# Attention sweep of an encoder layer: maxima turned in another PSUM bank and later in the group, one-over-sums products moved to the last group of four, and VectorE's order written out

## The chip, the cores and the metric

The kernel runs on one core of one Trainium2 chip. The metric is the device time of one execution in microseconds, taken as the median of several runs. The profile is that of one further execution. Its engines are called PE (TensorE), DVE (VectorE), ACT (ScalarE), POOL (GpSimd) and SP (SyncE, which issues most DMAs).

## The reference, cut to what matters

The program is one layer of an encoder: grouped-query attention over 1024 tokens, and then a mixture of 32 experts. The change lies in the attention alone.

```
qkv = x @ w_qkv                       # 16 query heads, 4 key/value heads, 64 wide
q, k = rope(rms_norm(q)), rope(rms_norm(k))
def query_block(q_blk):               # 128 queries at a time
    s = einsum('bqkgd,bskd->bkgqs', q_blk, k) * scale
    p = softmax(s, axis=-1)
    return einsum('bkgqs,bskd->bqkgd', p, v)
x = layer_norm(ALPHA * x + o @ w_o)
x = layer_norm(ALPHA * x + moe_ffn(x))   # top 4 of 32 experts
```

## The kernel before

The program has four stages: the projections to q, k and v (up to about 162 us), the attention sweep (to about 519 us), the output projection with layer norm and router (to about 760 us), and the experts.

The sweep runs over 32 groups n = 4i + g: block i of 128 queries (0 to 7), key/value head g (0 to 3), four query heads each. A group goes through eight steps k = 0 to 7, one for each tile of 128 keys. In step k PE makes the scores of this tile (`st`, two matmuls, function `probs`): the first multiplies the keys with the queries, the second multiplies a tile `q2` that holds the queries and, in four more rows, the negated maxima of each query. ACT takes the exponential into `pt` (L444), and POOL adds the `pt` of a group up into `acc` (L448), all but the last, which DVE adds (`late_sum`, L452).

The maxima must be known a group ahead. So in the same step PE makes half of a tile of scores the other way round (`sc`, function `scores`) for group n + 2, and DVE reduces each whole tile to its maxima `nm` (L434), four reductions in a group. `maxima_a` (L147, L148) turns the `nm` of group n + 1 with a PE transposition into a PSUM tile `tpm`, and a DVE product writes it into the four rows of `q2`. `maxima_b` (L153) has ACT copy the queries into `q2`.

After step 3 of a group, PE multiplies the `pt` of the group before with the values (`pv`, 32 matmuls into `po`), and ACT copies `po` out to `ot` (`close_a`, L469). In groups with g = 1 and 2 PE also turns half of the next block's queries (`stack_q`, tile `tpq`, L163) ahead of `pv`; ACT and DVE write the result into `qs`. In groups with g = 0 PE adds the four `acc` of the block before over the keys (`scale_a`, tile `su`) after `pv`, and DVE makes one-over-sums from it (L479 to L484, ending in `rr`). In groups with g = 1 PE spreads `rr` over the partitions (`scale_b`, tile `rb`, after steps 5 and 7), DVE multiplies `ot` with it (L492), and SP writes `ot` to memory (`od`, L494).

PSUM is full: `st` has two banks, `sc` two tiles of two banks, and one bank each is left for the tag `tp` and the tag `po`. In the tag `tp` stand `tpm`, `tpq`, `su` and `rb`, one at a time: each waits until the last reader of the one before is done. `po` has its bank alone.

PE's order in the sweep is written out by hand (`manual_schedule`, the loop below); DVE's, ACT's, POOL's and SP's orders are set by a scheduler when the program is built. Every matmul stands at L55.

Of the kernel before, what the change touches and what calls it, by code (L numbers as in the profile page):

```python
# [9 lines left out]
F32 = mybir.dt.float32  # L10
# [10 lines left out]
P = 128  # L21
# [6 lines left out]
HD = 64  # L28
# [17 lines left out]
def trunk_kernel(ctx: ExitStack, tc: tile.TileContext, x, w_qkv, q_norm, k_norm, w_o,  # L46
                 lnm_g, lnm_b, lnf_g, lnf_b, r_w, r_b, w_gu, b_gu, w_dn, b_dn,
                 rope_c, rope_s, out):
    nc = tc.nc
# [4 lines left out]
    def mm(o, lhsT, rhs, start=True, stop=True):  # L54
        nc.tensor.matmul(o, lhsT=lhsT, rhs=rhs, start=start, stop=stop)  # L55
# [49 lines left out]
    vn = p_kv.tile([P, NT, NKV, HD], F32, name="vn")  # L105
# [35 lines left out]
        if s == 7:  # L141
            nc.vector.tensor_reduce(nms[0], nms.pop("h"), AX.X, ALU.min)

    def maxima_a(n, ps):

        tp = ps.tile([P, 4, P], F32, tag="tp", name=f"tpm{n}")
        nc.tensor.transpose(tp[0:4, 0, :], nms.pop(n).bitcast(F32), ident)  # L147
        nc.vector.tensor_tensor(q2s[n % 3][HD:HD + 4], tp[0:4, 0:1, :].to_broadcast([4, 4, P]),  # L148
                                ident[0:4, 0:4, None].to_broadcast([4, 4, P]), ALU.mult)

    def maxima_b(n):
        i, g = divmod(n, NKV)
        nc.scalar.copy(q2s[n % 3][0:HD], qs[i][0:HD, 4 * g:4 * g + 4, :].bitcast(F32))  # L153

    def stack_q(i, h, ps):

        if h == 0:
            qs[i] = p_xq.tile([P, NH, P], F32R, tag="cols", bufs=2, name=f"qs{i}")
        qv = qs[i][:, 8 * h:8 * h + 8, :].rearrange("p (j a) t -> p j a t", a=2)
        tp = ps.tile([P, 4, P], F32, tag="tp", name=f"tpq{i}_{h}")  # L160
        for c in range(4):
            j = 4 * h + c
            nc.tensor.transpose(tp[:, c, :], ql[i][:, j * P:(j + 1) * P], ident)  # L163
        odd = p_xq.tile([P, 4, P], F32R, tag="odd", name=f"odd{i}_{h}")
        nc.scalar.copy(qv[0:HD, :, 0, :], tp[0:HD])
        nc.scalar.copy(odd[HD:P], tp[HD:P])
        nc.vector.tensor_tensor(qv[HD:P, :, 0, :], tp[0:HD], qv[0:HD, :, 0, :].bitcast(F32), ALU.subtract)
        nc.vector.tensor_tensor(qv[HD:P, :, 1, :], tp[HD:P], odd[HD:P].bitcast(F32), ALU.subtract)
        nc.scalar.copy(qv[0:HD, :, 1, :], odd[HD:P].bitcast(F32))
# [4 lines left out]
    with tc.tile_pool(name="p1", bufs=1, side="right", reuse_waits="tile") as p1, \  # L174
# [34 lines left out]
        def proj(i, k, j):  # L209
            hi, lo = xTs[i]  # L210
            sl = slice(j * 512, (j + 1) * 512)
            mm3(qkvs[i][j], hi[:, k, :], lo[:, k, :], wh[k][:, sl], wl[k][:, sl], k == 0, k == KD - 1)

        def open_qkv(i):
            t = {j: ps1.tile([P, 512], F32, tag=f"qkv{j}", name=f"qkv{i}_{j}") for j in (0, 2, 1)}
            qkvs[i] = [t[j] for j in range(3)]
# [4 lines left out]
        pe_order = ExitStack()  # L221
# [76 lines left out]
        def take_q(i, j):  # L298
            if j == 0:
                qcs[i] = rot("wr", [P, QKV], 3)  # L300
            qc = qcs[i][:, j * 512:(j + 1) * 512]
            if i == NT - 1 and j == 1:
                nc.scalar.copy(qc, qkvs[i][j])
                norms(qc, sums[i][:, 8 * j:8 * j + 8])
                return
            norms(qkvs[i][j], sums[i][:, 8 * j:8 * j + 8])
            nc.scalar.copy(qc, qkvs[i][j])
# [13 lines left out]
        for i in range(NT):  # L321
            k0 = (KD, late)[i] if i < 2 else 0
            if i > 1:
                open_qkv(i)
            for k in range(k0, KD):
                proj(i, k, 2)
            if 1 < i < NT - 1:
                turn_x(i + 1)
            norm_k(i)
            if i == NT - 1:  # L330
                stack_q(0, 0, ps1)
                stack_q(0, 1, ps1)
            for k in range(k0, KD):
                proj(i, k, 0)
                if i == NT - 1 and k % 2 == 1:
                    first_scores(k // 2, ps1)
            take_q(i, 0)
            if i == 0:
                take_q(i, 1)
            turn_k(i)  # L340
            if i == 0:
                turn_x(2)
            norm_q(i, 0)
            for k in range(k0, KD):
                proj(i, k, 1)
                if i == NT - 1 and 0 < k < 5:
                    first_scores(k + 3, ps1)
                if i == NT - 1 and k == 6:
                    maxima_a(0, ps1)
                    maxima_b(0)  # L350
            if i > 0:
                take_q(i, 1)
            norm_q(i, 1)
            if i == 1:
                in_order.close()
# [61 lines left out]
    with tc.tile_pool(name="p2", bufs=1, side="right", reuse_waits="tile") as p2, \  # L417
# [4 lines left out]
        pts, po, ot, sc, accs, rrs = [{} for _ in range(6)]  # L422
        NG = NT * NKV
# [30 lines left out]
        def pv(n):  # L454

            i, g = divmod(n, NKV)
            po[n] = ps_o.tile([P, 2, P], F32, tag="po", name=f"po{n}")
            for k in range(NT):
                for a in range(2):
                    mm(po[n][a * HD:(a + 1) * HD].rearrange("p j t -> p (j t)"), vn[:, k, g, :],  # L460
                       pts[n, k][:, 2 * a * P:(2 * a + 2) * P], k == 0, k == NT - 1)
            for k in range(NT):
                del pts[n, k]

        def close_a(n):
            i, g = divmod(n, NKV)
            if g == 0:
                ot[i] = p2.tile([P, KD, P], F32, tag="ot", bufs=2, name=f"ot{i}")
            nc.scalar.copy(ot[i][:, 2 * g:2 * g + 2, :], po.pop(n))  # L469

        def scale_a(i):

            su = ps_t.tile([P, 4, P], F32, tag="tp", name=f"su{i}")
            for m in range(4):
                for g in range(NKV):
                    mm(su[g * NE:(g + 1) * NE, 0, :], which[:, m].rearrange("p r m -> p (r m)"),
                       accs[NKV * i + g][:, m * P:(m + 1) * P], m == 0, m == 3)
            rs = p2.tile([P, P], F32, tag="rs", bufs=1, name=f"rs{i}")
            nc.vector.reciprocal(rs, su[:, 0, :])  # L479
            hi = p2.tile([P, P], F32R, tag="rh", bufs=1, name=f"rh{i}")  # L480
            nc.vector.tensor_copy(hi, rs)
            nc.vector.scalar_tensor_tensor(rs, hi.bitcast(F32), low, rs, ALU.mult, ALU.subtract)
            rrs[i] = p2.tile([P, KD, P], F32R, tag="rr", bufs=1, name=f"rr{i}")
            nc.vector.tensor_tensor(rrs[i], rs[:, None, :].to_broadcast([P, KD, P]),  # L484
                                    col.rearrange("p g j -> p (g j)")[:, :, None].to_broadcast([P, KD, P]), ALU.mult)
# [39 lines left out]


        pe_order = ExitStack()
        pe_order.enter_context(tc.manual_schedule(engines={mybir.EngineType.PE}))
        for n in range(NG + 1):
            i, g = divmod(n, NKV)  # L530
            for k in range(NT):
                if k == (6 if n == 0 else 2) and n + 1 < NG:
                    maxima_a(n + 1, ps_t)
                if n < NG:
                    probs(n, k)
                if n == 0:
                    for m in range(2):
                        scores(1 + k // 4, k % 4, m)
                elif n + 2 < NG:
                    scores(n + 2, k // 2, k % 2)  # L540
                if n < NG and i + 1 < NT and g == 0 and k == 6:
                    load_q(i + 1)
                if k == (7 if n == 0 else 3) and n + 1 < NG:
                    maxima_b(n + 1)
                if k == 3 and n > 0:
                    if g in (1, 2) and i + 1 < NT:
                        stack_q(i + 1, g - 1, ps_t)
                    if n < NG - 1:
                        late_sum(n - 1)
                    pv(n - 1)  # L550
                    close_a(n - 1)
                    if g == 0:
                        scale_a(i - 1)
                if i > 0:
                    if (g, k) == (1, 5) or n == NG and k == 5:
                        scale_b(i - 1, 0)
                    if (g, k) == (1, 7) or n == NG and k == 7:
                        scale_b(i - 1, 1)
            if i in (2, 3) and g == 2:
                load_o(i - 2)  # L560
            if i == 4 and g == 2:
                load_xr(0)
# [790 lines left out]
    for i in range(NT // 2):  # L1353
        f = slot(order[(len(seq) + 1 + i) % len(order)], f"fs{i}")
# [13 lines left out]
    with tc.tile_pool(name="gen", bufs=1, side="right", reuse_waits="tile") as gp, \  # L1368
# [5 lines left out]
        with tc.For_i(0, n_blk, 1) as b:  # L1374
# [33 lines left out]
            for n in range(4):  # L1408
                w = gp.tile([P, KD, 512], F32, tag="gw", bufs=2, name=f"gwg{n}")
                nc.sync.dma_start(w, w_gu[ds(ev, 1), :, n * 512:(n + 1) * 512].rearrange("o (k p) n -> p (o k) n", p=P))  # L1410
                ps = gps.tile([P, 512], F32, tag="gu", bufs=2, name=f"ggu{n}")
# [6 lines left out]
            for n in range(2):  # L1418
                w = gp.tile([P, KD, 512], F32, tag="gw", bufs=2, name=f"gwd{n}")
                nc.sync.dma_start(w, w_dn[ds(ev, 1), :, n * 512:(n + 1) * 512].rearrange("o (k p) n -> p (o k) n", p=P))  # L1420
                ps = gps.tile([P, 512], F32, tag="gu", bufs=2, name=f"gy{n}")
# [87 lines left out]
```

## Time and profile before

| | us |
|---|---|
| median of 3 runs | 2079.25 |
| lowest and highest of them | 2078.68, 2081.83 |
| profiled execution, its own time | 2075.34 |
| its span, first to last instruction | 2073.5 |
| PE busy in the span | 2011.8 (97%) |
| DVE busy in the span | 1601.8 (77%) |

The profiled execution is a little faster than the three timed runs. Its span is what the trace covers; its time has 1.8 us more around it. Busy shares of PE hide little waits, since a matmul's end is modelled; the starts of consecutive matmuls and the idle time shown in brackets tell more.

### The profile page before, as it was taken

How to read it: one execution, taken by the hardware profiler on the slowest of the kernel's cores; microseconds unless marked ns; L12 is line 12 of the kernel's file. 1: busy time of each engine (PE TensorE's matmuls, PEld its weight loads, DVE VectorE, ACT ScalarE, POOL GpSimd, SP SyncE). 2: the span in 40 equal slices, each digit the busy share in tenths (PEclk: the TensorE clock that was granted, in tenths of full speed). 3: DMA queues.
4: the chain of work that ended last, by engine and by line, in shares of the span. 5: the costliest groups of instructions: out<-in, count | busy, mean ns of one | idle time of the engine just before them, and what ended most of it. 6: DMA issues, size and time to landing. Idle time of an engine off the chain costs nothing. (4 is left out here: it accounts for less than half of the span.)

```text
span 2073.5 us, 28716 instructions
## 1 busy us (share of the span) xinstructions
PE 2011.8 (97%) x10691; PEld 1419.5 (68%) x10691; DVE 1601.8 (77%) x1649; ACT 1282.0 (62%) x1566; POOL 538.2 (26%) x373
## 2 busy tenths in 40 slices
PE   8998999999997999999999999999999999999997
PEld 6775666665675666666666767767777677677774
DVE  6647777776887877767777878878878788887894
ACT  5655655654554656566666766667667676676774
POOL 1216777775144211111102111101021121010100
PEclk9999999999998999999999999999999999999999
DMA  5216000000645777888788898978989889789875
GB/s 174 72 62 178 31 32 21 32 21 21 228 149 211 276 287 271 298 294 291 285 315 312 347 338 304 377 289 342 338 319 354 310 315 367 284 346 337 329 314 183
DMA packets 106352, 500.44 MB, mean 241 GB/s; under 512 B 16001, under 2 KB 17026, under 8 KB 73442
## 3 DMA queue, kind: packets, MB, share of 16 engines
q1 hardware_dynamic: 87360, 447.02, 56.0%
q0 software_dynamic: 16000, 50.90, 9.0%
q8 instruction: 85, 1.39, 0.3%
q10 hardware_dynamic: 2850, 0.66, 0.2%
q14 instruction: 57, 0.47, 0.1%
HBM read 457.05 MB, written 41.49 MB: 240 GB/s over the span
## 5 line engine op out<-in xcount | busy, mean ns | idle before, releaser
L55 PE MATMUL gu<-wh,xTh 128*128 128x512 f32 x1024 | 415.3, 406 | 1.0 <-ACT xTh L63 1.0
L55 PE MATMUL gu<-wh,xTl 128*128 128x512 f32 x1024 | 410.1, 400 | 0.0
L55 PE MATMUL gu<-wl,xTh 128*128 128x512 f32 x1024 | 401.9, 393 | 0.0
L1299 POOL DMA_INDIRECT fd<-y,mi x32 | 79.1, 2472 | 655.4 <-ACT y L1298 655.4
L448 POOL TENSOR_TENSOR acc<-acc,pt 128x512 f32<-128x512 f32 x152 | 211.8, 1394 | 78.3 <-ACT pt L444 68.7
L55 PEld LDWEIGHTS gu<-wh,xTh 128*128 128x128 f32 x1024 | 193.3, 189 | 42.4 <-ACT xTh L63 1.7
L55 PEld LDWEIGHTS gu<-wl,xTh 128*128 128x128 f32 x1024 | 193.3, 189 | 39.6 <-issue 0.2
L55 PEld LDWEIGHTS gu<-wh,xTl 128*128 128x128 f32 x1024 | 193.7, 189 | 38.8 <-issue 3.6
L55 PE MATMUL yp<-wl,aTh 128*128 128x512 f32 x512 | 204.2, 399 | 0.4 <-DVE wl L612 0.4
L55 PE MATMUL yp<-wh,aTh 128*128 128x512 f32 x512 | 201.6, 394 | 0.0
L55 PE MATMUL yp<-wh,aTl 128*128 128x512 f32 x512 | 199.7, 390 | 0.0
L434 DVE TENSOR_REDUCE nm<-sc 128x1 fp32r<-128x1024 f32 x124 | 150.6, 1221 | 50.5 <-PE sc L55 49.5
L444 ACT ACTIVATE pt<-st 128x512 f32<-128x512 f32 x256 | 149.4, 596 | 55.9 <-PE st L55 46.3
L598 POOL DMA_INDIRECT xg<-xd,mi x32 | 53.4, 1670 | 298.5 <-PE tpx L1136 288.9
L55 PE MATMUL qkv<-wh,xT 128*128 128x512 f32 x384 | 123.9, 403 | 2.6 <-ACT xT L63 1.4
L55 PEld LDWEIGHTS yp<-wh,aTh 128*128 128x128 f32 x512 | 96.2, 188 | 33.6 <-ACT act L1180 14.3
L55 PE MATMUL po<-pt,vn 128*64 128x256 f32 x1024 | 117.6, 382 | 0.0
L55 PE MATMUL st<-qs,kT_hi 128*128 128x512 f32 x256 | 112.5, 440 | 2.9 <-ACT pt L444 2.2
L55 PEld LDWEIGHTS yp<-wl,aTh 128*128 128x128 f32 x512 | 96.3, 188 | 21.9 <-DVE wl L612 1.2
L55 PEld LDWEIGHTS yp<-wh,aTl 128*128 128x128 f32 x512 | 96.1, 188 | 19.5
L55 PE MATMUL st<-q,kT_lo 128*128 128x512 f32 x256 | 102.2, 399 | 1.3 <-DVE q L148 1.3
L55 PE MATMUL sc<-kT_hi,qs 128*128 128x512 f32 x256 | 101.9, 404 | 1.0 <-DVE nm L434 0.8
(520 smaller groups left out, 4159.0 us busy)
## 6 DMA issues: line engine op xcount, KB each, us to landing
w0g<-in_expert_w_gate_up SPq DMA_DIRECT2D x8, 1024.0 KB, 7.1
w1g<-in_expert_w_gate_up SPq DMA_DIRECT2D x8, 1024.0 KB, 7.6
w2g<-in_expert_w_gate_up SPq DMA_DIRECT2D x8, 1024.0 KB, 9.6
w3g<-in_expert_w_gate_up SPq DMA_DIRECT2D x8, 1024.0 KB, 8.6
w4g<-in_expert_w_gate_up SPq DMA_DIRECT2D x8, 1024.0 KB, 6.9
w5g<-in_expert_w_gate_up SPq DMA_DIRECT2D x8, 1024.0 KB, 7.4
w6g<-in_expert_w_gate_up SPq DMA_DIRECT2D x8, 1024.0 KB, 6.5
w7g<-in_expert_w_gate_up SPq DMA_DIRECT2D x8, 1024.0 KB, 7.1
```

What stands on the lines that cost most here:

```text
L55: nc.tensor.matmul(o, lhsT=lhsT, rhs=rhs, start=start, stop=stop)
L434: nc.vector.tensor_reduce(nms[n][:, m:m + 1], sc.pop((n, m)), AX.X, ALU.max, negate=True)
L444: nc.scalar.activation(pts[n, k], st, AF.Exp)
L448: (nc.vector if n == NG - 1 or n == NG - 2 and k > 3 else nc.gpsimd).tensor_tensor(accs[n], pts[n, 0] if k == 1 else accs[n], pts[n, k], A ...
L598: return nc.gpsimd.indirect_dma_start(out=xg[e], out_offset=None, in_=xd, in_offset=bass.IndirectOffsetOnAxis(ap=mi[:, e:e + 1] if rows is ...
L1299: nc.gpsimd.indirect_dma_start(out=fd, out_offset=bass.IndirectOffsetOnAxis(ap=mi[:, e:e + 1], axis=0), in_=y, in_offset=None, bounds_chec ...
```

## The change

Three things are changed in the attention sweep. First, `tpm` takes its PSUM tile from the tag `po` instead of `tp`, and the transposition and its DVE product stand at step 5, after `pv`, instead of step 2, ahead of it (in the first group they stay at step 6). `po` tiles are made four columns of 128 wide so that both kinds have one shape; `pv` uses the first two. Second, `scale_b` moves from g = 1 (steps 5 and 7) to g = 3 (steps 1 and 5), two groups later, and the DVE product that makes `rr` is split off as `scale_c` and issued at step 7 of g = 0. Third, DVE's order in the sweep is written too: it is now the order of the calls in the loop. No instruction is added or removed; ACT's and POOL's orders come out the same.

```diff
-    def maxima_a(n, ps):
-
-        tp = ps.tile([P, 4, P], F32, tag="tp", name=f"tpm{n}")
+    def maxima_a(n, tp):
+
         nc.tensor.transpose(tp[0:4, 0, :], nms.pop(n).bitcast(F32), ident)
...
-            po[n] = ps_o.tile([P, 2, P], F32, tag="po", name=f"po{n}")
+            po[n] = ps_o.tile([P, 4, P], F32, tag="po", name=f"po{n}")
...
             nc.vector.scalar_tensor_tensor(rs, hi.bitcast(F32), low, rs, ALU.mult, ALU.subtract)
+            rrs[i] = rs
+
+        def scale_c(i):
+            rs = rrs[i]
             rrs[i] = p2.tile([P, KD, P], F32R, tag="rr", bufs=1, name=f"rr{i}")
             nc.vector.tensor_tensor(rrs[i], rs[:, None, :].to_broadcast([P, KD, P]),
...
-        pe_order.enter_context(tc.manual_schedule(engines={mybir.EngineType.PE}))
+        pe_order.enter_context(tc.manual_schedule(engines={mybir.EngineType.PE, mybir.EngineType.DVE}))
         for n in range(NG + 1):
             i, g = divmod(n, NKV)
             for k in range(NT):
-                if k == (6 if n == 0 else 2) and n + 1 < NG:
-                    maxima_a(n + 1, ps_t)
+                if k == (6 if n == 0 else 5) and n + 1 < NG:
+
+                    maxima_a(n + 1, ps_o.tile([P, 4, P], F32, tag="po", name=f"tpm{n + 1}"))
...
-                if k == (7 if n == 0 else 3) and n + 1 < NG:
+                if n == 0 and k == 7:
                     maxima_b(n + 1)
+                if k == 7 and g == 0 and 0 < n < NG:
+                    scale_c(i - 1)
                 if k == 3 and n > 0:
                     if g in (1, 2) and i + 1 < NT:
                         stack_q(i + 1, g - 1, ps_t)
+                    if n + 1 < NG:
+                        maxima_b(n + 1)
...
                     if g == 0:
                         scale_a(i - 1)
+                    if n == NG:
+                        scale_c(i - 1)
                 if i > 0:
-                    if (g, k) == (1, 5) or n == NG and k == 5:
+                    if (g, k) == (3, 1) or n == NG and k == 5:
                         scale_b(i - 1, 0)
-                    if (g, k) == (1, 7) or n == NG and k == 7:
+                    if (g, k) == (3, 5) or n == NG and k == 7:
                         scale_b(i - 1, 1)
```

How the instructions stand, in group 13 (block 3, g = 1). On PE, before, from the turning of the maxima of group 14 to the turning of the next block's queries (in the names the first number is the group and the second the step; for `tpq` it is the block and the half; the last number is the buffer's):

```order
L147 MATMUL tpm14_2878<-ident_70,nm14_2763 4x128
L55 MATMUL st13_2_2881<-qs3_2491,kT_hi_105 128x512
L55 MATMUL st13_2_2881<-q2_1_1558,kT_lo_106 128x512
L55 MATMUL sc15_1_2887<-kT_hi_105,qs3_2491 128x512
L55 MATMUL st13_3_2889<-qs3_2491,kT_hi_105 128x512
L55 MATMUL st13_3_2889<-q2_1_1558,kT_lo_106 128x512
L55 MATMUL sc15_1_2887<-kT_hi_105,qs3_2491 128x512
L163 MATMUL tpq4_0_2899<-ident_70,ql4_2852 128x128 x4
```

The same transposition on PE in the changed kernel, with the last matmuls of `pv` and step 4 ahead of it and step 5 behind it:

```order
L55 MATMUL po12_2908<-pt12_7_2855,vn_107 64x256 x2
L55 MATMUL st13_4_2927<-qs3_2487,kT_hi_105 128x512
L55 MATMUL st13_4_2927<-q2_1_1558,kT_lo_106 128x512
L55 MATMUL sc15_2_2933<-kT_hi_105,qs3_2487 128x512
L146 MATMUL tpm14_2935<-ident_70,nm14_2763 4x128
L55 MATMUL st13_5_2938<-qs3_2487,kT_hi_105 128x512
L55 MATMUL st13_5_2938<-q2_1_1558,kT_lo_106 128x512
```

The transposition `tpm` moved from between steps 1 and 2 to between steps 4 and 5, behind `pv`, and `tpq` no longer follows it.

DVE's order before, in the same group: the product `q2` out of `tpm14` stands between two reductions, and ahead of the last addition to group 12's sums and the products out of `tpq`.

```order
L434 TENSOR_REDUCE nm15_2876<-sc15_0_2867 128x1
L148 TENSOR_TENSOR q2_2_1560<-tpm14_2878,ident_70 4x512
L434 TENSOR_REDUCE nm15_2876<-sc15_1_2887 128x1
L452 TENSOR_TENSOR acc12_2753<-acc12_2753,pt12_7_2857 128x512
L167 TENSOR_TENSOR qs4_2898<-tpq4_0_2899,qs4_2898 64x4x128
L168 TENSOR_TENSOR qs4_2898<-tpq4_0_2899,odd4_0_2904 64x4x128
L434 TENSOR_REDUCE nm15_2876<-sc15_2_2936 128x1
```

DVE's order in the changed kernel, in the same group, from the product `rr` that now ends the group before:

```order
L487 TENSOR_TENSOR rr2_2859<-rs2_2818,col_120 128x1024
L433 TENSOR_REDUCE nm15_2876<-sc15_0_2867 128x1
L433 TENSOR_REDUCE nm15_2876<-sc15_1_2884 128x1
L166 TENSOR_TENSOR qs4_2894<-tpq4_0_2895,qs4_2894 64x4x128
L167 TENSOR_TENSOR qs4_2894<-tpq4_0_2895,odd4_0_2900 64x4x128
L451 TENSOR_TENSOR acc12_2753<-acc12_2753,pt12_7_2855 128x512
L147 TENSOR_TENSOR q2_2_1560<-tpm14_2935,ident_70 4x512
L433 TENSOR_REDUCE nm15_2876<-sc15_2_2933 128x1
```

The product out of `tpm14` now stands behind the two reductions, the products out of `tpq` and the addition to `acc12`.

PE's matmul of one-over-sums, before, in group 13 (`rb2_1` follows step 7 of it):

```order
L55 MATMUL st13_5_2938<-q2_1_1558,kT_lo_106 128x512
L55 MATMUL sc15_2_2936<-kT_hi_105,qs3_2491 128x512
L55 MATMUL rb2_0_2946<-rr2_2826,half_126 128x512
L55 MATMUL st13_6_2949<-qs3_2491,kT_hi_105 128x512
L55 MATMUL st13_6_2949<-q2_1_1558,kT_lo_106 128x512
```

The same matmul in the changed kernel (`rb2_1` follows step 5 of this group):

```order
L55 MATMUL st15_1_3069<-q2_0_112,kT_lo_106 128x512
L55 MATMUL sc17_0_3067<-kT_hi_105,qs4_2894 128x512
L55 MATMUL rb2_0_3078<-rr2_2859,half_126 128x512
L55 MATMUL st15_2_3081<-qs3_2487,kT_hi_105 128x512
L55 MATMUL st15_2_3081<-q2_0_112,kT_lo_106 128x512
```

It moved from group 13 (g = 1) to step 1 of group 15 (g = 3).

## Rows read from the trace of the kernel before

**Rows 1.** Busy time by stretch: PE, PEld, DVE, ACT, POOL, clock, DMA share, GB/s.

```profile
760.00:2073.00 1313.00, 1298.77 (x6715) 920.54 (x6713) 1037.41 (x740) 852.11 (x639) 188.25 (x89) 1.00 0.84 314
```

**Rows 2.** Who waited for whom, PE, 160 to 520 us: total, times, longest.

```profile
PE tpq L163 <- DVE q L148: 7.4, 14, 2.8
PE tpm L147 <- DVE nm L434: 3.9, 7, 0.6
...
PE rb L55 <- DVE ot L492: 2.7, 7, 0.4
```

**Rows 3.** PE in order of time, groups 11 and 12: start, duration, instructions.

```profile
292.37 3.67 PE L55 MATMUL po<-pt,vn 128*64 128x256 f32 x32
295.97 0.51 PE L55 MATMUL st<-qs,kT_hi 128*128 128x512 f32 x1
...
298.97 0.48 PE L55 MATMUL st<-qs,kT_hi 128*128 128x512 f32 x1
...
300.45 0.27 PE L147 MATMUL tpm<-ident,nm 128*4 128x128 f32 x1
300.64 0.50 PE L55 MATMUL st<-qs,kT_hi 128*128 128x512 f32 x1
```

**Rows 4.** ACT in order of time at the start of group 12.

```profile
299.49 0.61 ACT L153 CAST q<-qs 64x512 fp32r<-64x512 f32 x1
300.00 1.08 ACT L444 ACTIVATE pt<-st 128x512 f32<-128x512 f32 x2
```

**Rows 5.** PE in order of time, from group 12 to group 15.

```profile
302.23 3.67 PE L55 MATMUL po<-pt,vn 128*64 128x256 f32 x32
305.83 1.08 PE L55 MATMUL su<-acc,which 128*32 128x128 f32 x32
306.85 0.50 PE L55 MATMUL st<-qs,kT_hi 128*128 128x512 f32 x1
...
312.09 0.27 PE L147 MATMUL tpm<-ident,nm 128*4 128x128 f32 x1 [0.60 <-DVE nm L434]
...
313.93 0.66 PE L163 MATMUL tpq<-ident,ql 128*128 128x128 f32 x4 [0.17 <-DVE q L148]
314.52 3.67 PE L55 MATMUL po<-pt,vn 128*64 128x256 f32 x32
...
321.82 0.50 PE L55 MATMUL rb<-rr,half 128*128 128x512 f32 x1 [0.40 <-DVE ot L492]
...
326.33 3.67 PE L55 MATMUL po<-pt,vn 128*64 128x256 f32 x32
...
336.34 3.67 PE L55 MATMUL po<-pt,vn 128*64 128x256 f32 x32
```

**Rows 6.** DVE in order of time, groups 12 to 15.

```profile
306.98 0.96 DVE L479 RECIPROCAL rs<-su 128x128 f32<-128x128 f32 x1 [0.20 <-PE su L55]
...
309.68 1.22 DVE L484 TENSOR_TENSOR rr<-rs,col 128x1024 fp32r<-128x1024 f32 x1
310.81 2.35 DVE L434 TENSOR_REDUCE nm<-sc 128x1 fp32r<-128x1024 f32 x2
313.19 0.68 DVE L148 TENSOR_TENSOR q<-tpm,ident 4x512 fp32r<-4x512 f32 x1
...
316.57 0.69 DVE L167 TENSOR_TENSOR qs<-tpq,qs 64x512 fp32r<-64x512 f32 x1
...
335.55 1.76 DVE L452 TENSOR_TENSOR acc<-acc,pt 128x512 f32<-128x512 f32 x1 [1.21 <-POOL acc L448]
```

**Rows 7.** PE in order of time, groups 1 and 2.

```profile
180.77 3.67 PE L55 MATMUL po<-pt,vn 128*64 128x256 f32 x32
...
194.25 3.67 PE L55 MATMUL po<-pt,vn 128*64 128x256 f32 x32
```

**Rows 8.** ACT in order of time, in group 12.

```profile
305.95 0.37 ACT L469 COPY ot<-po 128x256 f32<-128x256 f32 x1 [3.24 <-PE po L55]
```

**Rows 9.** DMA issues: issuer, count, KB each, median us to landing.

```profile
od<-ot SPq DMA_DIRECT2D x8, 512.0 KB, 2.6
```

More of the change, by code (lines that the diff above doesn't have):

```diff
@@ L348, in trunk_kernel @@
                 if i == NT - 1 and k == 6:
-                    maxima_a(0, ps1)
+                    maxima_a(0, ps1.tile([P, 4, P], F32, tag="tp", name="tpm0"))
                     maxima_b(0)
@@ L456, in pv @@
             i, g = divmod(n, NKV)
-            po[n] = ps_o.tile([P, 2, P], F32, tag="po", name=f"po{n}")
+            po[n] = ps_o.tile([P, 4, P], F32, tag="po", name=f"po{n}")
             for k in range(NT):
                 for a in range(2):
-                    mm(po[n][a * HD:(a + 1) * HD].rearrange("p j t -> p (j t)"), vn[:, k, g, :],
+                    mm(po[n][a * HD:(a + 1) * HD, 0:2, :].rearrange("p j t -> p (j t)"), vn[:, k, g, :],
                        pts[n, k][:, 2 * a * P:(2 * a + 2) * P], k == 0, k == NT - 1)
@@ L468, in close_a @@
                 ot[i] = p2.tile([P, KD, P], F32, tag="ot", bufs=2, name=f"ot{i}")
-            nc.scalar.copy(ot[i][:, 2 * g:2 * g + 2, :], po.pop(n))
+            nc.scalar.copy(ot[i][:, 2 * g:2 * g + 2, :], po.pop(n)[:, 0:2, :])
         def scale_a(i):
```

## The prediction

> **What bounds the kernel now.** I read the busy time by stretch first. In the expert stage PE works 1298.77 of 1313.00 us [rows 1], and nothing in that stage is timed from the program's start, so what the attention sweep gives back should arrive at the end whole. PE is the engine to watch in the sweep too; the question is where it stands still there.
>
> The list of PE's waits in the sweep answers it [rows 2]. Three waits, all for DVE, come from the parts that the change touches: the turning of queries `tpq` waits for the product that empties `tpm` (7.4 us in 14), the turning of maxima `tpm` waits for the last reduction to `nm` (3.9 us in 7), and the second one-over-sums matmul `rb` waits for the product that empties the first (2.7 us in 7). That is 14.0 us, 0.7% of the program.
>
> Next comes PE in order of time, to learn what a group costs when nothing waits. From the `pv` of group 11 to that of group 12 [rows 3, 5]: `pv` 3.60 us (292.37 to 295.97), steps 4 to 7 3.00 us (to 298.97; I call this the tail), steps 0 to 3 of the next group with the `tpm` in them 3.26 us (to 302.23; the head). Together 9.86. The groups that wait are 12.29 (302.23 to 314.52), 11.81 (to 326.33) and 10.01 us apart (to 336.34). This pattern of four repeats for blocks 1 to 6, so a price found here counts six times.
>
> **The change part by part.** *The waits.* In its new bank `tpm` no longer stands in the way of `tpq`. The last reader of the tag `tp` is then, in g = 1, the reciprocal (306.98 in [rows 6], seven us ahead of the `tpq` at 313.93 in [rows 5]), and in g = 2 the products of the group before. At step 5 `tpm` needs maxima that were reduced a group earlier, so its 0.60 us wait [rows 5] has nothing to wait for. The two `rb` are four steps and a `pv` apart, so the 0.40 us between them [rows 5] goes as well.
>
> *The transposition's own time.* It takes 0.19 us of PE (300.45 to 300.64 [rows 3]). At the old place this cost nothing: ACT, which copies queries into `q2` at each group's start, begins the exponentials of steps 0 and 1 at 300.00 and has them both done at 301.08, the first at about 300.6 [rows 4]. PE's step 2, at 300.64, needs the `st` bank which that first one empties. Take `tpm` away and step 2 still starts at 300.64; I count no gain there (the bound is a gain of 0.19). At the new place no copy delays ACT, and the matmuls behind it are pushed back. The nearest row says 0.19, and I take 0.2 for each of 30 transpositions. The lower bound is 0, if the tail has the same cover as the head; the upper 0.6, if it meets a wait as long as the longest now [rows 2].
>
> *The matmuls `rb`.* A tail is twelve matmuls in 3.00 us, 0.25 each [rows 3]. Two leave the tail of g = 1. In g = 3 the first goes between steps 1 and 2, where `tpm` was, and 0.19 of it is covered (0.06); the second follows step 5 and costs 0.25.
>
> *The new handshake.* `tpm` must now wait until ACT has copied `po` out, and the next `pv` until DVE has emptied `tpm`. ACT's copy starts 0.12 us after `pv` gives way to the next work (305.83 [rows 5]) and takes 0.37 [rows 8]; step 4, 0.75 us of PE, lies between. Cost 0, and without step 4 about 0.5. The `pv` that follows is seven steps away.
>
> *DVE's order.* The tight place follows `su`. From the reciprocal on, DVE has now to do: reciprocal, two small operations and a reduction (2.70 us, 306.98 to 309.68 [rows 6]), the `tpm` product 0.68, a reduction 1.17, `rr` 1.22, two reductions 2.35, two products out of `tpq` at 0.69, the last addition to `acc` 1.76, and the next `tpm` product 0.68, each from a row of [rows 6]. That is 11.94 us and ends at 318.9. With the times below, group 14 starts at 320.7 and its second matmul needs that product. So 1.8 us are to spare and I count 0. In the groups without `su` DVE has 1.6 to 2.8 us less to do.
>
> *The addition that waits for POOL.* Before, DVE stood 1.21 us at it, at 335.55, with reductions behind it [rows 6]. Now two reductions always stand ahead of it, and the second can't start before step 3's matmuls are done. Here that is about 336.3, where `pv` starts [rows 5], 0.8 us after POOL's end, so the wait itself should go. The Trainium skill ("PSUM — Partial Sum Buffer", section Engine vs sequencer instructions) says that VectorE's queue is strictly first in, first out, which speaks against a written order: whatever stands behind a waiting addition is held too. The trace agrees that the reductions were held in that 1.21 us; by the rule the change costs nothing as long as the wait is shorter than the spare time, which the sum takes, and turns into the rival below when it is longer.
>
> *SP.* The write `od` is issued two groups later and the load of the next queries now stands ahead of it. It lands in 2.6 us [rows 9], and the buffer that it reads is written again more than a group later, at least 10 us. Cost 0; uncovered it would be 2.6 for each block.
>
> **The sum.** For one block: from g = 0 to g = 1, `pv` 3.60 + `su` 1.02 (305.83 to 306.85) + tail 3.00 + 0.20 + head 3.26 + `tpq` 0.59 (313.93 to 314.52) = 11.67 instead of 12.29 [rows 5], -0.62. From g = 1 to 2: 3.60 + 3.20 + 3.26 + 0.59 = 10.65 instead of 11.81, -1.16. From g = 2 to 3: 3.60 + 3.20 + 3.26 + 0.06 = 10.12 instead of 10.01, +0.11. From g = 3 to 0: 3.60 + 3.20 + 0.25 + 3.26 = 10.31 instead of 9.86, +0.45. Sum -1.22, six times: -7.3.
>
> Block 0 has the longest wait, 2.8 us [rows 2]. Its groups 1 and 2 are 13.48 apart [rows 7] and come to 10.65, -2.83; the two groups after pay 0.05 and 0.20: -2.6. Block 7 has no `tpq`: it loses one `tpm` wait and one `rb` wait (some 0.4 each) and two `rb` in g = 1 (0.5), and pays three transpositions and a `rb` (0.85): about -0.5.
>
> In all -10.4 us. The profiled execution's 2075.34 would become 2064.9; the three timed runs have a median 3.9 us higher, and against it the forecast is 2079.25 - 10.4 = 2068.9.
>
> **The rivals.** *The transposition isn't free at its new place.* For this speaks that no copy of ACT's makes slack in the tail, and that the `st` behind the transposition shows 0.50 us, like the one behind `pv` with 0.51, where the one at 298.97 shows 0.48 [rows 3]. Against it, the same transposition in the head takes 0.19. At 0.4 each, 6.0 us more are paid than in the sum: 2074.9. At the bound of 0.6 it is 12.0 more: 2080.9, no change. A measurement of this kernel tells about 0.2%, 4.2 us, from nothing, so from 0.41 on the result reads "same".
>
> *Everything is covered.* If the tail hides the transposition as the head did, 30 x 0.2 = 6.0 more is saved: 2062.9.
>
> *DVE becomes the bound behind `su`* (the other side). The mechanism is the spare 1.8 us above: if DVE's 11.94 us grow past 13.7, the second matmul of each g = 2 group waits for the product, in seven blocks. For a loss of 4.2 us each would have to lose (10.4 + 4.2) / 7 = 2.1 us, so the stretch would be 15.8 instead of 11.9. An addition held by POOL for 1.21 us is not enough; two such and POOL slowed by DVE's additions could be. At that point: 2083.5.
>
> *The change does nothing*, because the waits removed reappear one matmul later at ACT. ACT's exponentials bound the head now [rows 4]; but `tpq`'s waits stand after step 3, behind all of them. Time 2079.
>
> **How the numbers follow.** The forecast, 2064 to 2074.9: 0.71. Full cover, about 2063: 0.10. The costly transposition, 2075 to 2081: 0.11. No effect, 2079: 0.02. DVE as the bound, 2083 and more: 0.06. The range reaches from full cover, 2063, into the second case, to 2076. Faster by over 0.2% means below 2075.1: 0.81; same 0.13; slower 0.06.
>
> **What would show it.** In the profile after: `tpq` and `rb` gone from the list of PE's waits, or under 1 us each; `tpm` starting 0.7 to 0.9 us behind the first `st` after `pv`, with no idle time for ACT's copy; `pv` starts 11.7, 10.7, 10.1 and 10.3 us apart in the pattern of four; step 2 of a group still 1.67 us behind step 0 (298.97 to 300.64 [rows 3]), with no `tpm` between; DVE without its wait for POOL's sums. The prediction is wrong if PE waits for `tpm`'s product at a group's start, if the tail is much longer than 3.2, or if the sweep ends 10 us sooner and the program does not.

## The result and the profile after

| | before | after |
|---|---|---|
| median, us | 2078.97 (4 runs) | 2060.53 (4 runs) |
| lowest and highest | 2077.38, 2081.83 | 2059.23, 2060.72 |
| profiled execution, its own time | 2075.34 | 2060.55 |
| its span | 2073.5 | 2058.7 |

The ratio is 0.9908, with an interval from 0.9891 to 0.9926: 18.4 us faster. The forecast was 10.4 us, to 2068.9, with a range down to 2063; the time lies below the range. How much faster depends on the runs taken of before: over several chips they spread from 2075 to 2082 us, but for one of 2094 and one of 4025, and its profiled execution lay at their lower end. Profile against profile the gain is 14.8 us. The same changed kernel timed again on another chip, beside 15 runs of before, gave 16.0 (below). So the gain is 15 to 18 us, against 10.4.

The page of the changed kernel has in its first part the span and each engine's busy time:

```profile
span 2058.7 us, 28689 instructions
...
PE 2009.5 (98%) x10691; PEld 1418.0 (69%) x10691; DVE 1591.9 (77%) x1649; ACT 1281.6 (62%) x1566; POOL 540.0 (26%) x373
```

PE has 2.3 us less busy time in a span that is 14.8 us shorter: what went is time in which it stood still. The list of PE's waits in the changed kernel, 150 to 510 us (us in total, times, longest), answers to [rows 2]:

```profile
PE st L55 <- ACT pt L443: 3.6, 11, 1.9
PE st L55 <- DVE q L147: 1.3, 1, 1.3
PE sc L55 <- DVE nm L433: 0.8, 1, 0.8
PE tpm L146 <- DVE nm L142: 0.4, 1, 0.4
PE sc L55 <- DVE qs L167: 0.2, 1, 0.2
```

All three waits that the forecast removed are gone: `tpq` and `rb` don't stand here, and the one `tpm` left (its `nm` comes from L142) is that of the sweep's start. What remains is 6.3 us, most of it for ACT's exponentials.

PE in order of time in the changed kernel, from group 11 to group 14 (start, duration, instructions); it answers to [rows 3, 5]:

```profile
284.12 3.67 PE L55 MATMUL po<-pt,vn 128*64 128x256 f32 x32
287.72 0.51 PE L55 MATMUL st<-qs,kT_hi 128*128 128x512 f32 x1
288.53 0.27 PE L146 MATMUL tpm<-ident,nm 128*4 128x128 f32 x1
288.56 0.48 PE L55 MATMUL st<-qs,kT_hi 128*128 128x512 f32 x1
...
290.97 0.47 PE L55 MATMUL st<-qs,kT_hi 128*128 128x512 f32 x1
...
292.64 0.50 PE L55 MATMUL st<-qs,kT_hi 128*128 128x512 f32 x1
...
294.24 3.67 PE L55 MATMUL po<-pt,vn 128*64 128x256 f32 x32
297.85 1.08 PE L55 MATMUL su<-acc,which 128*32 128x128 f32 x32
298.86 0.50 PE L55 MATMUL st<-qs,kT_hi 128*128 128x512 f32 x1
...
301.96 0.43 PE L55 MATMUL st<-qs,kT_hi 128*128 128x512 f32 x1
...
305.68 3.67 PE L55 MATMUL po<-pt,vn 128*64 128x256 f32 x32
309.28 0.50 PE L55 MATMUL st<-qs,kT_hi 128*128 128x512 f32 x1
310.09 0.27 PE L146 MATMUL tpm<-ident,nm 128*4 128x128 f32 x1
310.12 0.48 PE L55 MATMUL st<-qs,kT_hi 128*128 128x512 f32 x1
...
312.33 0.46 PE L55 MATMUL st<-qs,kT_hi 128*128 128x512 f32 x1
...
316.17 3.67 PE L55 MATMUL po<-pt,vn 128*64 128x256 f32 x32
```

Three things are to be seen. Behind `tpm` the next matmul starts after 0.03 us (288.53 to 288.56, 310.09 to 310.12), where before it was 0.19 (300.45 to 300.64 [rows 3]). The tail of a group is 3.05 us (309.28 to 312.33) or 3.10 (298.86 to 301.96), and 3.25 with a `rb` in it (287.72 to 290.97); the forecast had 3.20 and 3.45. And the head still takes 3.27 (290.97 to 294.24), with step 2 still 1.67 behind step 0 (290.97 to 292.64).

| us from `pv` to `pv`, blocks 1 to 6 | g = 0 to 1 | 1 to 2 | 2 to 3 | 3 to 0 | sum |
|---|---|---|---|---|---|
| before | 12.29 | 11.81 | 10.01 | 9.86 | 43.97 |
| forecast | 11.67 | 10.65 | 10.12 | 10.31 | 42.75 |
| after | 11.44 | 10.49 | 10.06 | 10.12 | 42.11 |

The measured rows are those of five of the six blocks, to 0.03 us; block 2 is some 0.16 longer in both kernels.

DVE in order of time in the changed kernel, behind the sums of block 2 (what stands in brackets is idle time before the instruction and what ended it); it answers to [rows 6]:

```profile
299.00 0.96 DVE L478 RECIPROCAL rs<-su 128x128 f32<-128x128 f32 x1 [2.24 <-PE su L55]
...
303.62 1.95 DVE L487 TENSOR_TENSOR rr<-rs,col 128x1024 fp32r<-128x1024 f32 x1
...
309.28 0.69 DVE L451 TENSOR_TENSOR acc<-acc,pt 128x512 f32<-128x512 f32 x1
310.40 0.68 DVE L147 TENSOR_TENSOR q<-tpm,ident 4x512 fp32r<-4x512 f32 x1 [0.42 <-PE tpm L146]
```

DVE is through this stretch 12.1 us after the reciprocal's start (299.00 to 311.08; forecast 11.94), and the `tpm` product waits for PE, not PE for it.

Where the gain arises can be followed from one `pv` to the next in the profiles. The first `pv` comes at 179.40 instead of 180.77 [rows 7], the last at 498.71 instead of 515.13: the sweep gives back 16.4 us. Behind it the program takes 1560.0 us to the end against 1558.4, which leaves 14.8.

### The profile page after: what moved, and what is told of

The parts are those of the page before. It is cut to its first block, busy times and chain, and to the rows that moved or that the text cites. A ratio compares the mean times of both kernels' runs of the same rounds, so it can differ in the third digit from the quotient of the medians.

```text
span 2058.7 us, 28689 instructions
## 1 busy us (share of the span) xinstructions
PE 2009.5 (98%) x10691; PEld 1418.0 (69%) x10691; DVE 1591.9 (77%) x1649; ACT 1281.6 (62%) x1566; POOL 540.0 (26%) x373
## 5 line engine op out<-in xcount | busy, mean ns | idle before, releaser
L447 POOL TENSOR_TENSOR acc<-acc,pt 128x512 f32<-128x512 f32 x152 | 200.3, 1318 | 70.7 <-ACT pt L443 61.0
```

What stands on the lines that cost most here:

```text
L447: (nc.vector if n == NG - 1 or n == NG - 2 and k > 3 else nc.gpsimd).tensor_tensor(accs[n], pts[n, 0] if k == 1 else accs[n], pts[n, k], A ...
```

## The experiments

The question left by this result is why the sweep gave 16.4 us where the sum said 10.4. My theory was that the transposition costs PE much less than the sum had it, so that the turning alone carries nearly all of the gain; the rival, that the surplus comes from the other parts, `rb`'s new place and above all DVE's written order, which ends its wait for POOL. The quoted texts number the theories, mine first. All medians stand beside runs of the kernel before on the same chip.

**The turning alone.** The kernel before, with `tpm` in the bank of `po` and at step 5; `rb` as it was, and DVE's order still the scheduler's, which came out anew.

```diff
-                if k == (6 if n == 0 else 2) and n + 1 < NG:
-                    maxima_a(n + 1, ps_t)
+                if k == (6 if n == 0 else 5) and n + 1 < NG:
+                    maxima_a(n + 1, ps_o.tile([P, 4, P], F32, tag="po", name=f"tpm{n + 1}"))
```

> Only the transposition of the maxima is changed: the other bank and step 5; the one-over-sums matmuls stay in g = 1, DVE's order stays the scheduler's. Theory 1 (the gain is the waits of tpq and tpm, and the transposition is nearly free at step 5): both waits go from the list, the second rb's 2.7 us stays, the four groups of a block take 42.4 to 42.8 us instead of 43.98, and the time is 11 to 15 us below the kernel before. Rival (the written order of DVE carries the part that the prediction missed): 8 us below or less, with tails of 3.2 us.

Measured: 2065.53 against 2078.58, ratio 0.9937 [0.9921, 0.9954], 13.0 us faster. The block takes 11.79 + 11.07 + 10.05 + 9.91 = 42.82 us, and the waits of `tpq` are gone. Most of the gain is this part. The `rb` still wait for each other, 2.0 us in 7, which is in the 11.07.

**The products `rb` alone.** The kernel before, with `scale_c` split off and `scale_b` moved to g = 3; DVE's order left to the scheduler.

```diff
+                if k == 7 and g == 0 and 0 < n < NG:
+                    scale_c(i - 1)
...
-                    if (g, k) == (1, 5) or n == NG and k == 5:
+                    if (g, k) == (3, 1) or n == NG and k == 5:
...
-                    if (g, k) == (1, 7) or n == NG and k == 7:
+                    if (g, k) == (3, 5) or n == NG and k == 7:
```

> Only the one-over-sums matmuls are moved to g = 3 and the product rr is split off. Theory 1: PE's wait of the second rb (2.7 us) goes, the waits of tpq (7.4 us) and tpm stay; 2 to 5 us below the kernel before. Rival (the two rb in g = 1 also push DVE back, so that tpq waits behind their products): tpq's wait falls too, to under 5 us, and the time is 6 us or more below.

Measured: 2134.01 against 2078.58, ratio 1.0272 [1.0251, 1.0292], 55.4 us slower, which no theory had. The two largest of PE's waits in it, 150 to 580 us, and PE around one of them:

```profile
PE tpm L147 <- DVE ot L496: 25.6, 6, 4.3
PE tpq L163 <- DVE q L148: 21.2, 14, 2.8
```

```profile
358.60 0.40 PE L55 MATMUL rb<-rr,half 128*128 128x512 f32 x1
363.25 0.37 PE L147 MATMUL tpm<-ident,nm 128*4 128x128 f32 x1 [4.26 <-DVE ot L496]
...
366.12 5.20 PE L55 MATMUL po<-pt,vn 128*64 128x256 f32 x32
```

DVE in the same stretch:

```profile
359.74 1.73 DVE L452 TENSOR_TENSOR acc<-acc,pt 128x512 f32<-128x512 f32 x1 [1.20 <-POOL acc L448]
361.39 1.21 DVE L434 TENSOR_REDUCE nm<-sc 128x1 fp32r<-128x1024 f32 x1
362.53 0.67 DVE L496 TENSOR_TENSOR ot<-ot,rb 128x512 f32<-128x512 f32 x1
```

`tpm` at its old place and in the old bank stands right behind `rb`, and can start only when DVE has multiplied `ot` with that `rb`. That product stands third in DVE's row, behind an addition that waits 1.20 us for POOL. PE is idle for 4.26 us, from 358.99 on. Only 0.75 of that is the rest of the wait for POOL (to 359.74); the other 3.5 are the addition, the reduction and the product themselves. The `pv` after it takes 5.20 us instead of 3.67. Busy time of PE, PEld, DVE, ACT and POOL, then the granted clock, ahead of 362 us and behind it:

```profile
352.50:362.00 9.50, 6.49 (x35) 4.08 (x31) 4.71 (x4) 4.48 (x8) 5.07 (x4) 1.00 0.00 1
362.50:369.00 6.50, 5.75 (x21) 3.55 (x23) 2.60 (x4) 1.20 (x2) 2.54 (x2) 0.50 0.00 0
```

PE had stood still since 358.99 when the clock fell from 1.00 (2.4 GHz) to 0.50 (1.2 GHz), and most of the slow `pv` runs at that level. PE's waits add up to 36 us more in this kernel's sweep than in the kernel before's, while the time from the first `pv` to the last is 57.6 us longer (392.0 against 334.4). So some 21 us stand in no wait; I estimate that most of them are instructions at the lower clock, which is 0.94 over this sweep and 0.99 over that of the kernel before.

This is the mechanism that the prediction weighed with the Trainium skill ("PSUM — Partial Sum Buffer", section Engine vs sequencer instructions, VectorE's queue is strictly first in, first out) and found harmless. The trace of this kernel agrees with the rule, at 4.26 us a time. In the changed kernel nothing waits for that product at once, since `tpm` has another bank.

**The same with DVE's order written.**

```diff
-        pe_order.enter_context(tc.manual_schedule(engines={mybir.EngineType.PE}))
+        pe_order.enter_context(tc.manual_schedule(engines={mybir.EngineType.PE, mybir.EngineType.DVE}))
```

> The one-over-sums matmuls moved to g = 3, alone, with DVE's order written, so that the addition that waits for POOL stands behind the product that empties the bank. Theory 1 (with rb alone moved, DVE was held by POOL in front of that product, and TensorE's clock fell in the waits): the wait of tpm for it falls from 4.3 us to about 2, the clock stays up in the sweep, and the time is 2076 to 2088. Rival (rb in g = 3 is bad in the shared bank whatever DVE's order): 2115 or more.

Measured: 2084.18 against 2077.27, ratio 1.0035 [1.0023, 1.0048], 6.9 us slower. PE's two largest waits, 150 to 540 us:

```profile
PE tpm L147 <- DVE ot L496: 10.1, 6, 1.7
PE tpq L163 <- DVE q L148: 9.7, 14, 2.3
```

The granted clock in the sweep is 0.99 here, 0.94 in the kernel without the order. With the product ahead of the addition the wait falls from 4.3 to 1.7 us, and nearly 50 of the 55 us go. The waits and the clock went together here; no run changes one without the other.

**DVE's order alone.** The kernel before with the same edit of one line.

> Only DVE's order is written, by the loop of the kernel before. Theory 1: the addition to acc now stands behind the tpm product, so the long wait of 2.8 us in block 0 falls to about 0.6; the other waits of tpq stay near 0.5 each. 1 to 4 us below the kernel before. Rival (the written order alone takes the waits away): tpq's waits in total under 2 us and 8 us or more below.

Measured: 2080.5 against 2078.58, ratio 1.0006 [0.9988, 1.0024]. No change, which neither theory had, but of gains and a loss. `tpm` no longer waits for `nm` (3.9 us before [rows 2]), and `tpq` waits 6.3 us in all, 0.5 at most. In their place the next `sc` waits, since `rr` now stands ahead of the reduction that frees its bank and no longer behind it. The groups of blocks 1 and 3 to 6 take 45.18 us instead of 43.97, while the three groups of block 0 take 30.72 instead of 33.33.

```profile
PE sc L55 <- DVE nm L434: 9.5, 8, 1.5
PE tpq L163 <- DVE q L148: 6.3, 14, 0.5
```

**The changed kernel without the order**, DVE's order left to the scheduler.

> The changed kernel with DVE's order left to the scheduler again. Theory 1: bank, step and rb carry the gain; the time stays within 2 us of the changed kernel's 2060.5 and the four groups of a block take 42.1 to 42.3 us. Rival (the order carries what was missed): 2064 us or more.

Measured: 2062.19 against 2078.58, ratio 0.9926 [0.991, 0.9943]. The block takes 42.45 us, 0.34 more than after; six `sc` wait for `nm`, 2.8 us in all, where one waits 0.8 with the order written. The expected 42.1 to 42.3 was a little missed. In blocks 1 to 6 the written order is worth 1.8 us.

**The changed kernel with `rb` back at g = 1**, steps 5 and 7.

> The changed kernel with the one-over-sums matmuls back in g = 1, at steps 5 and 7. Theory 1 (their move is worth the wait between the two, 0.3 to 0.4 us a block, and a little cover): the second rb waits again, some 2 us in 7, g = 1 to 2 takes 11.0 instead of 10.5 and g = 3 to 0 9.9 instead of 10.1; 2 to 4 us slower than the changed kernel. Rival (it is worth nothing once the banks are apart): within 1 us of it.

Measured: 2062.01 against 2077.27, ratio 0.9928 [0.9912, 0.9945]. The block takes 11.44 + 11.07 + 10.06 + 9.91 = 42.48, 0.37 more than after, and the `rb` wait for each other again, 2.0 us in 7. In blocks 1 to 6 that is 2.1 us. Beside the same runs of the kernel before stood **the changed kernel again**:

> The changed kernel as it is, beside the kernel before on one chip, for the size of the change. Theory 1 (the sweep is 16.4 us shorter and what follows it keeps its length but for the place of the low-clock stretches): 15 to 19 us below. Rival (the first result overstated it by the spread of the kernel before): 10 to 14 us below.

Measured: 2061.28, ratio 0.9927 [0.9911, 0.9944]. By the medians `rb`'s move is worth 0.7 us, less than the two medians' own spread; the 2.1 us are read from the trace alone.

**The transposition twice.** The changed kernel, with a second transposition of the same maxima into columns that nothing reads.

```diff
+        if n > 0:
+            nc.tensor.transpose(tp[0:4, 1, :], nms[n].bitcast(F32), ident)
         nc.tensor.transpose(tp[0:4, 0, :], nms.pop(n).bitcast(F32), ident)
```

> The changed kernel with each transposition of the maxima made twice, the first into columns that nobody reads. Theory 1 (the transposition is hidden at step 5, because ACT's exponentials pace steps 4 to 7): the tail stays at 3.05 to 3.15 us and the time rises by 0 to 3 us. Rival (the prediction's price, 0.2 us each, is right and something else gave the rest): the tail rises by 0.2 and the time by 5 to 7 us.

Measured: 2063.95 against 2077.42, ratio 0.9932 [0.9914, 0.995]. The groups are 11.53, 10.60, 10.17 and 10.23 apart: each is 0.09 to 0.11 longer than after, and the 30 that were added behind a `pv` come to some 3 us. PE in one tail of it:

```profile
289.90 0.27 PE L147 MATMUL tpm<-ident,nm 128*4 128x128 f32 x1
290.01 0.27 PE L148 MATMUL tpm<-ident,nm 128*4 128x128 f32 x1
290.03 0.48 PE L55 MATMUL st<-qs,kT_hi 128*128 128x512 f32 x1
```

A second transposition costs 0.10 us, half of the price in the sum. The first costs no more: tails with it take 3.05 to 3.11, without it 3.00.

**ACT's order written, in the kernel before.** This moves the copy of the queries (the CAST of [rows 4]) from the start of a head to the time of `pv`, and nothing else: the other instructions of ACT, and those of DVE and POOL, keep their order.

```diff
-        pe_order.enter_context(tc.manual_schedule(engines={mybir.EngineType.PE}))
+        pe_order.enter_context(tc.manual_schedule(engines={mybir.EngineType.PE, mybir.EngineType.Activation}))
```

> The kernel before with ACT's order alone written. Theory 1 (the copy of queries paces the head there too, and hid the transposition): heads of groups without tpq fall from 3.26 to 3.1 to 3.2 us, because the transposition now costs its own 0.1 there; 2 to 5 us below the kernel before. Rival (heads are paced by PE in the kernel before): no change.

Measured: 2075.09 against 2077.27, ratio 0.9991 [0.9981, 1.0]. PE in a head of it:

```profile
298.72 0.48 PE L55 MATMUL st<-qs,kT_hi 128*128 128x512 f32 x1
...
300.20 0.27 PE L147 MATMUL tpm<-ident,nm 128*4 128x128 f32 x1
300.23 0.48 PE L55 MATMUL st<-qs,kT_hi 128*128 128x512 f32 x1
...
301.81 0.87 PE L55 MATMUL po<-pt,vn 128*64 128x256 f32 x6
```

ACT's copy now stands behind `pv`'s start:

```profile
302.17 0.61 ACT L153 CAST q<-qs 64x512 fp32r<-64x512 f32 x1
```

This settles the price. With the copy out of the way, the matmul behind the very same `tpm`, at the old place and in the old bank, starts 0.03 us after it instead of 0.19; the head falls from 3.26 to 3.09. The 0.19 was ACT's delay. The time moves little here: the groups with a `tpq` still take 12.29 and 11.82, since `tpq` waits 7.7 us in all for DVE whatever the head does, and only the other two fall, to about 9.67 each (one of twelve took 9.93).

**ACT's order written, in the changed kernel.**

> The changed kernel with ACT's order in the sweep written out as well, by the order of the calls; this moves ACT's copy of the queries into q2 from the start of each group to the time of pv, when ACT is idle. Theory 1 (the head is paced by ACT, and that copy costs 0.2 to 0.3 us of it): heads fall from 3.26 to 3.0 to 3.1 us, 5 to 8 us less in all, 2052.5 to 2055.5. Rival (PE's own work paces the head): heads stay within 0.05 and the time within 2 us of 2060.5.

Measured: 2055.48 (2053.86 to 2056.09) against 2077.42, ratio 0.9893 [0.9876, 0.9909]. It is the fastest of all: the block takes 41.33 us, 0.78 less than after, with heads of 3.06 in g = 3 (288.76 to 291.82) and the copy behind the last exponential, in `pv`'s time:

```profile
291.04 1.25 ACT L443 ACTIVATE pt<-st 128x512 f32<-128x512 f32 x2 [0.18 <-PE st L55]
292.19 0.61 ACT L152 CAST q<-qs 64x512 fp32r<-64x512 f32 x1
```

Set beside the run before it, this prices the transposition at its old place: with the copy away, the same head takes 3.09 with a `tpm` in it and 3.06 without.

**The changed kernel with the old bank** (step 5, tag `tp`):

> The changed kernel with the maxima's transposition at step 5 but in its old bank, with tpq, su and rb. Theory 1 (the step behind pv takes the wait of tpq away, whatever the bank): tpq still doesn't wait; in g = 0 the transposition waits some 0.3 us for the reciprocal and in g = 3 the second rb some 0.3 for its product, 2 to 6 us slower than the changed kernel. Rival (the bank carries the gain): 8 us slower or more.

Measured: 2065.51 against 2077.42, ratio 0.9942 [0.9925, 0.9958], some 4 to 5 us behind the changed kernel. The `tpm` of g = 0 waits for the reciprocal (1.3 us in 7), `tpq` no longer waits, and a block takes 42.79: 0.34 more than after from g = 0 to 1, and 0.34 more from g = 3 to 0, where the second `rb` now follows `tpm` in the same bank. The list shows no wait for the second of these.

**The changed kernel with the old step** (the new bank, step 2):

> The changed kernel with the maxima's transposition in the new bank but at step 2. Theory 1 (the step matters): now pv must wait until DVE has emptied the bank; in g = 1, where DVE is latest, by 1 to 2 us, elsewhere by 0 to 0.4; 8 to 16 us slower than the changed kernel. Rival (the bank carries the gain): within 3 us of it.

Measured: 2072.83 against 2077.42, ratio 0.9978 [0.9968, 0.9988], 12 us behind the changed kernel. The wait has moved to `pv`, which needs the bank that `tpm`'s product has yet to empty:

```profile
PE po L55 <- DVE q L147: 13.5, 21, 1.8
```

So, each taken back alone, the step is worth some 12 us and the bank 4 to 5, and neither does it all.

## Why the prediction was wrong

The direction and the waits that go were right; the time lay under the range because one term was too large, one was left out, and the executions lay apart.

**The step that failed** is the price of the transposition: "At the new place no copy delays ACT, and the matmuls behind it are pushed back. The nearest row says 0.19, and I take 0.2 for each of 30 transpositions." Measured, the matmul behind it starts 0.03 us later, a tail with it takes 3.05 to 3.11 instead of 3.00, and doubling it costs 0.10. The sentences ahead of the quoted ones hold the mistake: they show that the `st` at 300.64 waits for ACT, whose exponential ends at about 300.6. The gap of 0.19 was then read once as cover, and once as the transposition's own time. It can't be both. Without the copy the gap is 0.03. At the lower price, four groups are shorter by 0.59 in their tails (0.10, 0.15, 0.14 and 0.20), which is nearly all of the 0.64 by which the block beats the forecast: 42.11 instead of 42.75, six times 3.9 us. Smaller errors cancel beside it: a `tpq` takes 0.53 and not 0.59, the head with a `rb` 3.42 and not 3.32.

**The rest of the 6 us** by which the sweep beat the sum: the first `pv`, 1.4 us sooner, which the sum had not at all; block 7, whose four groups lose 0.9 (30.73 to 29.80 from the `pv` of g = 0 to that of g = 3) and not 0.5; and block 0, 2.9 and not 2.6. What stands behind the 1.4 can be read at the sweep's start, from its first `st` to the first `pv`. That takes 18.67 us before (162.10 to 180.77) and 16.39 after (163.01 to 179.40), where the changed kernel reaches the sweep 0.91 later. With `rb` alone, whose change begins later in the sweep, and with the clock at 1.00 as after, it takes 17.22 (163.51 to 180.73). So 0.8 of the 1.4 belong to the change, and 0.43 of these are a wait for `tpq` that [rows 2] already counts among its 14. The other 1.5 us by which this stretch is shorter go with the clock, 0.53 before and 1.00 after, and 0.9 of them are taken back by the later arrival: that part is luck.

**From the sweep to the time.** The sweep beat the sum by 6.0 us, the measured gain by 8.0. Behind the sweep the changed kernel took 1.6 us longer, and the profiled execution of the kernel before lay 3.6 below the median of its four runs, that of the changed kernel at its own. This last part belongs to the runs and to no step of the sum; with the 16.0 us of the repeated timing most of it is gone.

**The rival "everything is covered"** came true in its number: it had 16.4 us, 2062.9, and a chance of 0.10. The sweep gave 16.4, part of it from the first `pv`, which the rival hadn't in it: that it met the number is partly luck. Its reason was only nearly right: the transposition isn't hidden, it is cheap. *The costly transposition* is refuted by the tail of 3.05.

**DVE as the bound** didn't happen. The stretch took 12.1 us, 0.2 over the forecast, though its parts were off in both directions: `rr` took 1.95 instead of 1.22, the last addition 0.69 instead of 1.76. The addition's wait for POOL, 1.21 at 335.55 [rows 6], is gone. It was one of 14 in the list of DVE's waits before, 195 to 480 us; the same list after has none:

```profile
DVE acc L452 <- POOL acc L448: 17.2, 14, 1.5
```

The mechanism is real all the same: in the kernel with `rb` alone it costs tens of us, at a place the prediction had not looked at, the tag `tp`.

**The steps that held.** `tpm`, `tpq` and `rb` no longer wait. The handshake is free: no `tpm` behind a `pv` waits for ACT's copy. The head kept 3.27 with step 2 at 1.67, as forecast, so ACT's copy bounded it and taking `tpm` away gave nothing there. What the sweep gave back arrived at the end but for 1.6 us.

**What each part does.** Of the 1.86 us that a block loses, the turning alone brings 1.15 (43.97 to 42.82). Taken out last, the move of `rb` is worth 0.37 and the written order 0.34. Put in first, `rb`'s move costs 55 us, and the order makes most blocks 1.2 us longer and block 0 2.6 shorter: both gain in blocks 1 to 6 only once the turning has left its old place.

## What to carry to other kernels

Take an instruction's price from a place where no other engine holds up what follows; a gap that you have just ascribed to ACT can't also be the price of the PE instruction in it, and doubling the instruction measures it directly. Parts of a change that lose when tried alone can gain together, when one frees the buffer that the other needs. A tile that waits behind another in a shared PSUM bank inherits everything that is queued on the reader's engine, so follow that queue before moving the tile.

## What the runs showed of the hardware

DVE's products and additions and POOL's additions slow each other. In the changed kernel the product `rr` takes 1.22 us at its shortest and 1.95 in the median, and the row of POOL that overlaps it, a single addition, takes 2.25 where 1.29 is usual:

```profile
293.58 1.29 POOL L447 TENSOR_TENSOR acc<-pt,pt 128x512 f32<-128x512 f32 x1
...
304.44 2.25 POOL L447 TENSOR_TENSOR acc<-pt,pt 128x512 f32<-128x512 f32 x1
```

The Trainium skill ("SBUF — State Buffer", section Who interferes with whom) says that a VectorE instruction with two inputs in SBUF contends with a GpSimd instruction that reads SBUF, and that the one issued later waits. The trace agrees: `rr` was issued at 303.62, while POOL's additions ran until 304.48, and 0.86 + 1.22 = 2.08 is near its 1.95. DVE's last addition is likewise 0.69 with POOL idle (at 318.90 in the changed kernel) and 1.76 beside POOL's (at 335.55 before [rows 6]).

The clock of the sweep's first microseconds differs from execution to execution. The busy time of each engine and, behind POOL, the granted clock, from 165 to 172 us, first of the kernel before, then of the changed kernel:

```profile
165.00:172.00 7.00, 5.83 (x15) 4.16 (x14) 5.42 (x9) 5.10 (x10) 4.91 (x7) 0.53 0.69 167
```

```profile
165.00:172.00 7.00, 5.12 (x21) 3.38 (x20) 6.18 (x11) 6.40 (x17) 4.08 (x6) 1.00 0.61 145
```

The clock of 1.00 is the level of 2.4 GHz throughout; 0.53 is nearly all at 1.2. PE is busy for 5.83 us with 15 matmuls in the one, and for 5.12 with 21 in the other. Over the fourteen profiles it lies between 0.51 and 1.00, with the transposition at either place. The changed kernel repeated had 0.85 there and took 17.35 us from the first `st` to the first `pv` instead of 16.39. And the kernel with `rb` alone, up to there the kernel before, had 1.00 and took 17.22 instead of 18.67:

```profile
165.00:172.00 7.00, 4.83 (x19) 3.37 (x20) 6.15 (x12) 6.47 (x19) 3.58 (x6) 1.00 0.53 130
```

So 1.0 and 1.5 us at the sweep's start belong to the execution and not to the kernel; what sets it was not found.
